# A hybrid encoder layer: the S5 phasors made during the projections and loaded in the attention loop

## The chip, the core and the metric

The kernel runs on one core of one Trainium2 chip. A core has five engines that work side by side, each through its own instructions in their order: TensorE (PE, matrix products; its weight loads are PEld), VectorE (DVE), ScalarE (ACT), GpSimd (POOL) and SyncE (SP), which here only issues DMAs. Engines wait for each other and for DMAs through semaphores; an instruction that waits holds up everything behind it on its engine. The metric is the device time of one execution in microseconds.

## The reference

One layer over 2048 positions of width 1024 (batch 1, depth 1). The normed input is projected once, and the columns are shared out among an attention branch, an S5 branch and their gates:

```
h = RMSNorm(x);  z = h @ w_in            # q 256, kv 128, k_rope 64, gate 512, u 512, gate 512
A = MLA attention, 4 heads, softmax over all 2048 positions
B = S5: 32 groups of 16 channels, 64 complex states each, forward and backward scan
    lam_bar = exp(lam * dt);  h_t = lam_bar * h_(t-1) + b_bar u_t;  y = Re(C h) + D u
B = gelu(B);  B = B * sigmoid(B @ w_glu + b_glu)
out = x + RMSNorm(concat(RMSNorm(A)*SiLU(gA), RMSNorm(B)*SiLU(gB)) @ w_out)
```

All is float32; products are made of three matmuls on split operands (`mm3`).

## The kernel before, in words

Every engine's order is written out by hand (`manual_schedule` for all five): what stands in the code is the order on each engine, and nothing is moved later.

**Projections** (about 0 to 380 us). The 16 position tiles go in pairs. For the pair starting at tile `s`, `blocks(s)` runs eight blocks of some 5.7 us on PE: z of the first tile, u (two), the attention gate `ga` (two), the S5 gate `gs` (two), z of the second tile; in the first and the last pair the two z blocks come first, side by side. After the seventh and eighth block `turn` transposes the next pair's two tiles into PSUM (`pt`, two buffers), and ACT and DVE copy each out as a rounded part `hh` and a rest `hl` (L195, L196). A gate block ends with a DVE operation `gst` (L330) and two stores. Each tile is normed with DVE `rv`, POOL `rr`, DVE `xt` (L188, L189, L268).

After each block from the second pair on, `step()` lets a generator go on with table work on DVE until a budget is used: each table operation charges 60 + its elements to a meter, each step takes `BUDGET` = 1800 off. The generator makes the rope tables first and then the S5 tables (`s5_params`), which it stores to `tab_d` in DRAM. There are 52 steps: eight in each of six pairs, four in the last.

**Attention loop** (about 395 to 1125 us). Steps `t` of some 2.7 us, eight to a unit (one head of 256 queries). In a step PE makes scores `sc` into one of two PSUM buffers (L1102 to L1106), transposes earlier probabilities (`pt`, L1150), and multiplies with the values (`av`); DVE takes the maximum (`nm`, L1107) and a rest `plo` (L1572); ACT takes the exponential `e` (L1113), which releases the scores' buffer, and the rounded copy `phi` (L1158). Into these steps the 32 S5 groups are woven, seven steps each (two take six), by `s5_pre` and `s5_post`. Every four groups form a set q with one table tile `tab` (two buffers), loaded from `tab_d` in the first step of the set before (`s5_load`, L858). In that set's third step `k_build(q)` issues 8 stores to `k_d` (L936, L937) and 8 loads `m` from it (L941).

In a group's third step POOL makes its phasors, cosine and sine over the 256 chunks, from four 16-element tables: two products (L971, L972) and, a step later, their sum (L975), into a tile `t` (`t3`, two buffers). In the fifth step ACT adds the negated copy (L984). DVE uses them two steps later (L997), POOL once more (L1018).

Then come the tail of the attention, the GLU and the output projection, which the change doesn't touch.

Of the kernel before, what the change touches and what calls it, by code (L numbers as in the profile page):

```python
# [11 lines left out]
F32 = mybir.dt.float32  # L12
# [4 lines left out]
ALU = mybir.AluOpType  # L17
# [28 lines left out]
LN2_2 = float(np.float32(math.log(2.0) - LN2_1))  # L46
GELU_C = math.sqrt(2.0 / math.pi)
GELU_A = 0.044715
BUDGET = 1800
MANUAL = {mybir.EngineType.PE, mybir.EngineType.Activation, mybir.EngineType.DVE, mybir.EngineType.Pool, mybir.EngineType.SP}  # L50


# [90 lines left out]
def bc(ap, dims):  # L143
    return ap.to_broadcast(dims)
# [3 lines left out]
def tile_hymba(ctx, tc, x, pos, inv_freq, pre_g, w_in, q_g, w_uqT, w_uqr, kv_g, w_ukT, w_uv, attn_g,  # L148
# [62 lines left out]
    for nm, m in ([("qr", T), ("qi", T)] + [(f"bt{i}", GH) for i in range(3)] + [("br", GH), ("bi", GH)]  # L211
# [2 lines left out]
        F[nm] = 4 * n_tab, m  # L214
        n_tab += m
    tab_d = dram.tile([P, NG // 4, 4 * n_tab], F32, tag="tab_d", name="tab_d")


    ph1, ph1a, ph1b, ph1g = (ExitStack() for _ in range(4))

    def pool(st, name, bufs, **kw):
        return st.enter_context(tc.tile_pool(name=name, bufs=bufs, reuse_waits="tile", **kw))
# [9 lines left out]
    s5t = pool(ph1g, "s5t", 7, side="right")  # L232
    xp = pool(ph1b, "xp", 2, side="right")
    s5p = pool(ph1b, "s5p", 1, side="right")
    psT = pool(ph1, "psT", 2, space=PSUM)
    psZ = pool(ph1, "psZ", 5, space=PSUM)
    psK = pool(ph1, "psK", 1, space=PSUM)
# [113 lines left out]
    def s5_params():  # L351
# [6 lines left out]
        def store(nm, ap):  # L358
            o, m = F[nm]
            G.dma_start(tab_d[:, :, o:o + 4 * m], ap.rearrange("p (q g) m -> p q (g m)", g=4))  # L360

        def neg(src, m):
            t_ = Scratch(s5t, [P, NG, m], "sc")()
            e.tensor_scalar(t_, src, -1.0, None, ALU.mult)
            return t_
# [85 lines left out]
        for nm, src in (("b", ph2), ("a", ph32)):  # L451
            hi, lo = new("hi" + nm), new("lo" + nm)
            e.tensor_scalar(hi, src, 1.5 * 2.0 ** 13, None, ALU.add)
            e.tensor_scalar(hi, hi, 1.5 * 2.0 ** 13, None, ALU.subtract)
            e.tensor_tensor(lo, src, hi, ALU.subtract)
            ang, rr = sp(), sp()
            ix = bc(idx[nm].unsqueeze(1), d3)
            e.tensor_tensor(ang, bc(hi.unsqueeze(2), d3), ix, ALU.mult)
            yield from reduce_angle(e, sp, rr, ang)
            e.tensor_tensor(ang, bc(lo.unsqueeze(2), d3), ix, ALU.mult)  # L460
            yield
            e.tensor_tensor(rr, rr, ang, ALU.add)
            yield
            if nm == "a":
                e.tensor_tensor(rr[:, :, 8:16], rr[:, :, 8:16], bc(phi.unsqueeze(2), [P, NG, 8]), ALU.add)
                r0, rr = rr, sp()
                yield from reduce_angle(e, sp, rr, r0)
            so, co = sp(), sp()
            yield from sincos(e, sp, so, co, rr)
            if nm == "a":  # L470
                e.tensor_copy(ep_r, co[:, :, 8])
                e.tensor_scalar(ep_i, so[:, :, 8], -1.0, None, ALU.mult)

            e.tensor_scalar(so[64:P], so[64:P], -1.0, None, ALU.mult)
            yield
            if nm == "b":
                store("bs", so)
                store("bc", co)
            else:
                store("aa3", so)  # L480
                store("aa2", co)
                store("aa1", neg(so, 16))
                store("aa0", neg(co, 16))
            yield

        br, bi = new("br", GH), new("bi", GH)
# [35 lines left out]
        yield from wait_steps(2)  # L522


        pc = psK.tile([P, 4, P], F32, tag="k", name="pc")
        rawn = neg(rawi, GH)
        yield from wait_steps(1)
# [8 lines left out]
        cst = Scratch(s5t, [P, 4, P], "sc")()  # L536
        for n in range(4):
            e.scalar_tensor_tensor(cst[:, n, :], ident, dsk[:, n:n + 1], pc[:, n, :], ALU.mult, ALU.add)
        for j in range(8):
            w = slice(GH * j, GH * j + GH)  # L540
            SP.dma_start(k_d[j::8, :, T, :].rearrange("n i h -> i n h"), cst[w, :, w])
# [6 lines left out]
        yield  # L548

    def tables():  # L550
        yield from rope_tables()
        yield from s5_params()

    gen = tables()

    def wait_steps(n):
        for _ in range(n):
# [3 lines left out]
    def step():  # L561

        VM.n -= BUDGET
        while VM.n < 0 and next(gen, "end") != "end":
            pass

    def blocks(s):

# [58 lines left out]
    for s in range(0, NT, 2):  # L627
        last = s + 2 == NT
        blk = blocks(s)
        for n in range(4 if last else 8):  # L630
# [13 lines left out]
                turn(xs[n - 6], n - 6)  # L644
            if s > 0:
                step()
    assert next(gen, "end") == "end"
    ph1b.close()
    ph1a.close()

# [299 lines left out]
    def group(g):  # L950

        q, i = divmod(g, 4)
        f = S5[q]

        uh, ul = (t_[:, :, i] for t_ in U)
        wt = s2.tile([P, 2, P], F32, tag="w", name="w")
        tmp = s2.tile([P, 2, P], F32, tag="tmp", name="tmp", bufs=2)
        two(G, wt, tmp, f["qr"][:, i, ::-1], f["qi"][:, i, ::-1], f["bt"][:, i, 1:3, :], f["bt"][:, i, 0:2, :])
        yield "pre"
        yield "post"  # L960
        G.tensor_tensor(wt, wt, tmp, ALU.add)
        yield "pre"
        yield "post"

        t3 = s2.tile([P, 3, 16, 16], F32, tag="t3", name="t3", bufs=2)
        t3b = s2.tile([P, 2, 16, 16], F32, tag="t3b", name="t3b")
        d = [P, 2, 16, 16]

        def b4(t):
            return bc(t[:, i, :].unsqueeze(1).unsqueeze(1), d)  # L970
        G.tensor_tensor(t3[:, 0:2], bc(f["aa"][:, i, 1:3, :].unsqueeze(3), d), b4(f["bc"]), ALU.mult)  # L971
        G.tensor_tensor(t3b, bc(f["aa"][:, i, 0:2, :].unsqueeze(3), d), b4(f["bs"]), ALU.mult)  # L972
        yield "pre"
        yield "post"
        G.tensor_tensor(t3[:, 0:2], t3[:, 0:2], t3b, ALU.add)  # L975
        t3 = t3.rearrange("p a b c -> p a (b c)")
        yield "pre"
        pw = psM.tile([P, 512], F32, tag="m", name="pw2")
        for ri in range(2):
            PE.transpose(pw[:, ri * P:(ri + 1) * P], wt[:, ri, :], ident)  # L980
        wh_, wl_ = (s2.tile([P, 256], F32R, tag=x_, name=x_) for x_ in ("wTh", "wTl"))
        split(wh_, wl_, pw[:, 0:256])
        yield "post"
        A.activation(t3[:, 2, :], t3[:, 0, :], AF.Copy, scale=-1.0)  # L984
        yield "pre"
        yield "post"
        yield "pre"
        px = psM.tile([P, 2, NC], F32, tag="m", name="px")
        for ri in range(2):
            w = slice(ri * P, (ri + 1) * P)  # L990
            mm3(px[:, ri, :], wh_[:, w], wl_[:, w], uh, ul, True, True)
        yield "post"
        d = [P, 2, NC]
        co, si = bc(t3[:, 1:2, :], d), t3[:, ::-2, :]
        ta = s2.tile(d, F32, tag="ta", name="ta")
        tb = s2.tile(d, F32, tag="tb", name="tb")
        V.tensor_tensor(ta, px, co, ALU.mult)  # L997
        V.tensor_tensor(tb, px[:, ::-1, :], si, ALU.mult)
        yield "pre"
        yield "post"  # L1000
        xm, gt = Xm[g % 2], Gt[g % 2]
        V.tensor_tensor(in_time(xm), of_tiles(ta), of_tiles(tb), ALU.add)
        yield "pre"
        yield "post"

        df = bc(f["rt"][:, i, :], [P, NC - 1])
        for r in range(2):
            o = r * NC
            V.tensor_tensor_scan(gt[0:64, o + 2:o + NC + 1], df[0:64], xm[0:64, r, 0:NC - 1], 0.0, ALU.mult, ALU.add)
            V.tensor_tensor_scan(gt[64:P, o + 1:o + NC][:, ::-1], df[64:P], xm[64:P, r, 1:][:, ::-1], 0.0,  # L1010
                                 ALU.mult, ALU.add)
            yield "pre"
            yield "post"
        g3 = gt[:, 1:2 * NC + 1].rearrange("p (a c) -> p a c", a=2)
        hc = s2.tile(d, F32, tag="hc", name="hc")
        tb2 = s2.tile(d, F32, tag="tb2", name="tb2")
        g4, co, si = in_time(g3), of_tiles(co), of_tiles(si)
        G.tensor_tensor(of_tiles(hc), g4, co, ALU.mult)  # L1018
        G.tensor_tensor(of_tiles(tb2), g4[:, ::-1], si, ALU.mult)
        yield "pre"  # L1020
        yield "post"
        G.tensor_tensor(hc, hc, tb2, ALU.subtract)
        yield "pre"
        yield "post"
        yield "pre"
        py = psY.tile([P, 2, P], F32, tag="y", name="py")
        mm3(py, M[0][:, i, :], M[1][:, i, :], uh, ul, True, False)
        yield "post"
        yield "pre"
        yield "post"  # L1030
        yield "pre"
        for ri in range(2):
            PE.matmul(py, f["v"][i][:, ri, :], hc[:, ri, :], start=False, stop=ri == 1)
        if i == 0:
            f["y"] = s1.tile([P, 2, 4, P], F32, tag="y4", name=f"y4_{q}")
        A.activation(f["y"][:, :, i, :], py, AF.Copy)
        if i == 3:
            for s8 in range(8):
                SP.dma_start(y_d[s8, q].rearrange("a (g h) c -> h (a g) c", g=4),
                             f["y"][s8 * GH:(s8 + 1) * GH].rearrange("h a g c -> h (a g) c"))  # L1040
        yield "end"
# [634 lines left out]
```

## Time and profile before

| | |
|---|---|
| median of 3 runs | 1387.77 us (1386.6 to 1389.01) |
| the profiled execution's own time | 1389.19 us |
| its span, first to last instruction | 1387.4 us |
| PE, DVE, ACT, POOL busy | 97%, 70%, 57%, 47% |
| chain that ended last, by engine | PE 78%, DVE 10%, ACT 4%, POOL 3%, DMA 1% |

A time is compared with the median. The profile is one execution, and durations and waits come from it. A busy share is a mean over stages with different limits, so a change is judged in the stage where it acts. A row of a timeline gives start, duration, engine, line, operation, the tiles as output<-input, and in square brackets the idle time before it and what ended it.

### The profile page before, as it was taken

The page shows a single profiled execution, that of the slowest core. Times are in us where ns is not written, and L with a number is a line of the kernel's source. Part 1 is how long each engine was busy: PE and PEld are TensorE (multiplying, and loading weights), DVE is VectorE, ACT ScalarE, POOL GpSimd, SP SyncE. Part 2 cuts the span into 40 slices and gives each one's busy share as a digit, 9 for nine tenths or more (in the row PEclk, how much of TensorE's full clock was granted, in tenths as well). Part 3 has the DMA queues.
Part 4 walks back from the last instruction along what each step waited for, and adds up shares of the span by engine and source line. Part 5 has one row for each costly group of instructions (what it writes and reads, how often), then busy time and mean ns, then how long its engine had stood idle before and what let it go on. Part 6 is the DMA issues. An engine that isn't in the chain of part 4 may idle for free.

```text
span 1387.4 us, 24305 instructions
## 1 busy us (share of the span) xinstructions
PE 1349.4 (97%) x9016; PEld 1219.0 (88%) x9016; DVE 974.4 (70%) x1812; ACT 797.4 (57%) x1828; POOL 647.7 (47%) x680
## 2 busy tenths in 40 slices
PE   7999999999989999999999999999999999999998
PEld 7999999999968888898888888888888887888886
DVE  6456554442388888887888788787887886767774
ACT  7312222222248778777778777777787785445442
POOL 2102320332357576565667655756641984333340
PEclk9999999999999999999999999999999999999999
DMA  8322323442630020201202021110101344455432
GB/s 299 88 54 76 83 68 83 87 123 62 157 83 21 27 45 9 51 24 29 46 5 63 12 45 31 28 39 10 29 9 43 105 116 110 141 171 167 130 106 92
DMA packets 122135, 102.93 MB, mean 74 GB/s; under 512 B 14672, under 2 KB 107104, under 8 KB 122016
## 3 DMA queue, kind: packets, MB, share of 16 engines
q1 hardware_dynamic: 110384, 89.43, 23.1%
q0 software_dynamic: 2272, 7.62, 2.2%
q10 hardware_dynamic: 9360, 4.33, 1.5%
q8 instruction: 70, 1.15, 0.4%
q14 instruction: 49, 0.40, 0.1%
HBM read 63.80 MB, written 37.54 MB: 73 GB/s over the span
## 4 chain that ended last, share of the span: by engine, by line
PE 78%; DVE 10%; ACT 4%; issue 3%; POOL 3%; DMA 1%; SPq 0%; POOLq 0%; ACTq 0%; DVEq 0%
PE pt L1150 6%; PE po L202 4%; PE po L203 4%; PE po L204 4%; PE sc L1102 3%; PE av L1170 3%; PE av L1171 3%; PE av L1172 3%; PE sc L1105 3%; PE sc L1103 3%; PE sc L1106 3%; PE sc L1104 3%; PE z_ga L203 2%; PE z_ga L204 2%; PE z_ga L202 2%
## 5 line engine op out<-in xcount | busy, mean ns | idle before, releaser
L1572 DVE TENSOR_TENSOR plo<-pt,phi 128x512 fp32r<-128x512 f32 x255 | 175.8, 689 | 80.9 <-ACT phi L1158 78.7
L1113 ACT ACTIVATE e<-sc,nm 128x512 f32<-128x512 f32 x256 | 176.8, 690 | 74.3 <-DVE nm L1107 73.2
L1158 ACT ACTIVATE phi<-pt 128x512 fp32r<-128x512 f32 x256 | 153.5, 600 | 80.7 <-PE pt L1150 79.2
L1107 DVE TENSOR_REDUCE nm<-sc 128x1 f32<-128x512 f32 x256 | 175.6, 686 | 25.8 <-PE sc L1106 22.3
L1170 PE MATMUL av<-phi,kn_h 128*128 128x256 f32 x512 | 165.2, 323 | 5.9 <-ACT avs L1175 5.9
L1142 ACT ACTIVATE e<-e,f 128x512 f32<-128x512 f32 x226 | 164.8, 729 | 1.5 <-DVE f L1131 1.5
L1150 PEld LDWEIGHTS pt<-ident,e 128*128 128x128 f32 x1024 | 127.4, 141 | 36.6 <-DVE e L1138 2.4
L1150 PE MATMUL pt<-ident,e 128*128 128x128 f32 x1024 | 154.5, 273 | 2.3 <-DVE e L1138 1.5
L1172 PE MATMUL av<-plo,kn_h 128*128 128x256 f32 x512 | 144.9, 283 | 0.4 <-DVE plo L1572 0.4
L1171 PE MATMUL av<-phi,kn_l 128*128 128x256 f32 x512 | 144.6, 283 | 0.0
L1102 PE MATMUL sc<-kT_h,qo 128*128 128x512 f32 x256 | 114.4, 447 | 6.6 <-ACT e L1113 4.9
L1018 POOL TENSOR_TENSOR hc<-G,t 128x512 f32<-128x512 f32 x32 | 41.7, 1304 | 153.5 <-DVE G L1010 140.0
L1170 PEld LDWEIGHTS av<-phi,kn_h 128*128 128x128 f32 x512 | 97.7, 191 | 8.5 <-ACT avs L1175 8.5
L202 PE MATMUL po<-woh,ah 128*128 128x512 f32 (+1 forms) x264 | 103.2, 391 | 1.9 <-ACT u L1409 1.9
L204 PE MATMUL po<-woh,al 128*128 128x512 f32 (+1 forms) x264 | 103.1, 390 | 0.0
L203 PE MATMUL po<-wol,ah 128*128 128x512 f32 (+1 forms) x264 | 103.0, 390 | 0.0
L1103 PE MATMUL sc<-kT_l,qo 128*128 128x512 f32 x256 | 101.2, 395 | 0.0
L1105 PE MATMUL sc<-krS,qo 128*128 128x512 f32 x256 | 101.0, 395 | 0.0
L1106 PE MATMUL sc<-krS,qo 128*128 128x512 f32 x256 | 100.9, 394 | 0.0
L1104 PE MATMUL sc<-kT_h,qo 128*128 128x512 f32 x256 | 100.2, 392 | 0.0
L1171 PEld LDWEIGHTS av<-phi,kn_l 128*128 128x128 f32 x512 | 97.5, 190 | 0.0
L1172 PEld LDWEIGHTS av<-plo,kn_h 128*128 128x128 f32 x512 | 96.6, 189 | 0.6 <-DVE plo L1572 0.6
(338 smaller groups left out, 4105.3 us busy)
## 6 DMA issues: line engine op xcount, KB each, us to landing
g_d<-gst SPq DMA_DIRECT2D x64, 128.0 KB, 2.0
g<-g_d SPq DMA_DIRECT2D x16, 512.0 KB, 5.9
xr<-in_x_dram SPq DMA_DIRECT2D x16, 512.0 KB, 6.5
xt<-in_x_dram SPq DMA_DIRECT2D x15, 512.0 KB, 3.8
out_dram<-res SPq DMA_DIRECT2D x15, 512.0 KB, 3.0
u_d<-ust ACTq DMA_DIRECT2D x64, 64.0 KB, 2.1
u<-u_d SPq DMA_DIRECT2D x64, 64.0 KB, 2.5
o_d<-o SPq DMA_DIRECT2D x32, 128.0 KB, 1.8
```

Source lines behind the costliest of these rows:

```text
L202: PE.matmul(ps, ahi, bhi, start=first, stop=False)
L203: PE.matmul(ps, ahi, blo, start=False, stop=False)
L204: PE.matmul(ps, alo, bhi, start=False, stop=last)
L1102: PE.matmul(ps, qo[:, 0, w], kT_h[:, c], start=True, stop=False)
L1107: V.tensor_reduce(st["nm"][:, qt, kb:kb + 1], ps, AX.X, ALU.max, negate=True)
L1113: A.activation(e, st.pop("s"), AF.Exp, bias=st["nm"][:, qt, kb:kb + 1], accum_out=st["L"][:, qt, kb:kb + 1])
L1142: A.activation(e, e, AF.Copy, scale=f)
L1150: PE.transpose(pt[:, kk, qt, :], st["e"][qt, kt // 4][:, o:o + P], ident)
L1170: PE.matmul(o, kn_h[:, kt, :], hi[:, w], start=kt == 0, stop=False)
L1171: PE.matmul(o, kn_l[:, kt, :], hi[:, w], start=False, stop=False)
L1172: PE.matmul(o, kn_h[:, kt, :], lo[:, w], start=False, stop=kt == NT - 1)
L1572: V.tensor_tensor(lo[0], lo[1], f32(lo[2]), ALU.subtract)
```

## The change

In the projections a second generator, `phasors`, makes the phasors of all 32 groups and stores them to a new DRAM tensor `ph_d`. For every set of four it loads the tables into a tile `pht`. For each group POOL makes one product into `ph`, DVE the other into PSUM (`phb`, in the single buffer of `psK`) and their sum into `ph`, and SP stores it, 256 KB. `ph` and `pht` have one buffer each. `step()` calls this generator once after the tables that it needs are stored, twice when the other generator has run dry, and not while `psK` is held by another product. The budget goes from 1800 to 2300, and the S5 tables come ahead of the rope tables.

In the attention loop the two products and the sum of a group go, and in their place SP loads the tile `t` from `ph_d`.

```diff
-BUDGET = 1800
+BUDGET = 2300
...
+    ph_d = dram.tile([NG, P, 2, 256], F32, tag="ph_d", name="ph_d")
...
+    php = pool(ph1b, "php", 1, side="right")
...
                 store("aa0", neg(co, 16))
+                made.append(True)
...
+        held.append(True)
         pc = psK.tile([P, 4, P], F32, tag="k", name="pc")
...
             e.scalar_tensor_tensor(cst[:, n, :], ident, dsk[:, n:n + 1], pc[:, n, :], ALU.mult, ALU.add)
+        held.clear()
...
     def tables():
+        yield from s5_params()
         yield from rope_tables()
-        yield from s5_params()
-
-    gen = tables()
+
+    made, held = [], []
+
+    def phasors():
+
+        d = [P, 2, 16, 16]
+        for q in range(NG // 4):
+            tb = php.tile([P, 5, 4, 16], F32, tag="pht", name="pht")
+            o = F["aa0"][0]
+            SP.dma_start(tb[:, 0:3].rearrange("p r g m -> p (r g m)"), tab_d[:, q, o:o + 192])
+            o = F["bc"][0]
+            SP.dma_start(tb[:, 3:5].rearrange("p r g m -> p (r g m)"), tab_d[:, q, o:o + 128])
+            yield
+            for i in range(4):
+                t2 = php.tile(d, F32, tag="ph", name="ph")
+                t2b = psK.tile(d, F32, tag="k", name="phb")
+
+                def b4(r):
+                    return bc(tb[:, r, i, :].unsqueeze(1).unsqueeze(1), d)
+                G.tensor_tensor(t2, bc(tb[:, 1:3, i, :].unsqueeze(3), d), b4(3), ALU.mult)
+                V.tensor_tensor(t2b, bc(tb[:, 0:2, i, :].unsqueeze(3), d), b4(4), ALU.mult)
+                V.tensor_tensor(t2, t2, t2b, ALU.add)
+                SP.dma_start(ph_d[4 * q + i], t2.rearrange("p r a c -> p r (a c)"))
+                if i < 3:
+                    yield
+
+    gen, phs = tables(), phasors()
...
     def step():
         VM.n -= BUDGET
         while VM.n < 0 and next(gen, "end") != "end":
             pass
+        for _ in range((bool(made) + (VM.n < 0)) * (not held)):
+            next(phs, None)
...
-        t3 = s2.tile([P, 3, 16, 16], F32, tag="t3", name="t3", bufs=2)
-        t3b = s2.tile([P, 2, 16, 16], F32, tag="t3b", name="t3b")
-        d = [P, 2, 16, 16]
-
-        def b4(t):
-            return bc(t[:, i, :].unsqueeze(1).unsqueeze(1), d)
-        G.tensor_tensor(t3[:, 0:2], bc(f["aa"][:, i, 1:3, :].unsqueeze(3), d), b4(f["bc"]), ALU.mult)
-        G.tensor_tensor(t3b, bc(f["aa"][:, i, 0:2, :].unsqueeze(3), d), b4(f["bs"]), ALU.mult)
+        t3 = s2.tile([P, 3, 256], F32, tag="t3", name="t3", bufs=2)
+        SP.dma_start(t3[:, 0:2, :], ph_d[g])
         yield "pre"
         yield "post"
-        G.tensor_tensor(t3[:, 0:2], t3[:, 0:2], t3b, ALU.add)
-        t3 = t3.rearrange("p a b c -> p a (b c)")
         yield "pre"
```

Two places show how instructions move. The first is DVE in the projections' seventh pair (tiles 12 and 13), from the norm of the second tile loaded (`rv`, `xt`) on; `gst` are the gates. Before:

```order
L188 TENSOR_SCALAR rv<-ss 128x1
L268 TENSOR_SCALAR xt_3451<-xt_3451,rr 128x1024
L68 TENSOR_SCALAR sc<-sc 128x512
L330 SCALAR_TENSOR_TENSOR gst<-tt,z_ga 128x512 x2
L68 TENSOR_SCALAR sc<-sc 128x512
L330 SCALAR_TENSOR_TENSOR gst<-tt,z_gs 128x512 x2
L196 TENSOR_TENSOR hl<-pt,hh 128x4x128 x2
```

DVE at the same place now:

```order
L188 TENSOR_SCALAR rv<-ss 128x1
L270 TENSOR_SCALAR xt_3615<-xt_3615,rr 128x1024
L579 TENSOR_TENSOR phb<-pht 128x512
L580 TENSOR_TENSOR ph<-ph,phb 128x512
L579 TENSOR_TENSOR phb<-pht 128x512
L580 TENSOR_TENSOR ph<-ph,phb 128x512
L332 SCALAR_TENSOR_TENSOR gst<-tt,z_ga 128x512
L579 TENSOR_TENSOR phb<-pht 128x512
L580 TENSOR_TENSOR ph<-ph,phb 128x512
L579 TENSOR_TENSOR phb<-pht 128x512
L580 TENSOR_TENSOR ph<-ph,phb 128x512
L332 SCALAR_TENSOR_TENSOR gst<-tt,z_ga 128x512
```

Two phasors now stand behind the second norm and behind each gate; from the first norm of this pair up to the transposed copies `hl` there are ten, in five steps, and six more follow in three steps. The sixteen phasors before them come one to a step.

The second place is SP at the first group of a set in the attention loop (set 6 here): `tab` the next set's tables, `k_d` and `m` the stores and loads of `k_build`, `o_d` the attention's output. Before:

```order
L858 DMA tab_10165<-tab_d 128x964
L936 DMA k_d<-ks 16x128
L937 DMA k_d<-ks 16x128
...
L941 DMA m_10269<-k_d 16x4x128 x8
L1182 DMA o_d<-o 128x2x128
```

SP at the same place now, `t` being the phasors:

```order
L891 DMA tab_10326<-tab_d 128x964
L969 DMA k_d<-ks 16x128
L970 DMA k_d<-ks 16x128
...
L974 DMA m_10430<-k_d 16x4x128 x8
L999 DMA t_10441<-ph_d 128x512
L1207 DMA o_d<-o 128x2x128
```

The load of the group's phasors stands behind the tables' load and the sixteen DMAs of `k_build`. It is so in the first group of sets 1 to 6; in set 7 there is no tables' load ahead.

## Rows read from the trace of the kernel before

**Rows 1.** Two stages: us; busy us of PE, PEld, DVE, ACT, POOL; PEclk; DMA share; GB/s.

```profile
100.00:330.00 230.00, 230.00 (x1775) 225.80 (x1773) 113.38 (x309) 51.96 (x120) 53.66 (x72) 1.00 0.35 87
396.00:1082.00 686.00, 671.72 (x4457) 593.36 (x4456) 561.90 (x1031) 521.83 (x1238) 416.05 (x433) 1.00 0.13 31
```

**Rows 2.** Waits of SP's queue: who waited for whom, us, times, longest.

```profile
SPq L858 <- DVE G L1010: 92.4, 6, 22.0
...
SPq L936 <- ACT ks L932: 12.2, 2, 11.5
```

**Rows 3.** Timeline of SP, first group of set 1.

```profile
481.90 0.34 SPq L858 DMA_DIRECT2D tab<-tab_d  x1
...
482.81 0.41 SPq L936 DMA_DIRECT2D k_d<-ks  x1
...
487.56 3.61 SPq L941 DMA_DIRECT2D m<-k_d  x8
```

**Rows 4.** Timeline of SP, first group of set 6.

```profile
897.35 3.62 SPq L941 DMA_DIRECT2D m<-k_d  x8
```

**Rows 5.** Timeline of ACT, first groups of sets 1 and 6.

```profile
486.33 0.42 ACT L984 ACTIVATE t<-t 128x256 f32<-128x256 f32 x1
...
487.32 0.68 ACT L1113 ACTIVATE e<-sc,nm 128x512 f32<-128x512 f32 x1
...
897.52 0.43 ACT L984 ACTIVATE t<-t 128x256 f32<-128x256 f32 x1
...
898.30 0.71 ACT L1113 ACTIVATE e<-sc,nm 128x512 f32<-128x512 f32 x1
```

**Rows 6.** Timeline of PE: scores two steps after those copies; a pause at 838.06.

```profile
491.36 0.40 PE L1102 MATMUL sc<-kT_h,qo 128*128 128x512 f32 x1
...
838.06 0.50 PE L1102 MATMUL sc<-kT_h,qo 128*128 128x512 f32 x1 [2.45 <-ACT e L1113]
...
902.72 0.39 PE L1102 MATMUL sc<-kT_h,qo 128*128 128x512 f32 x1
```

**Rows 7.** Stretches behind that pause, columns as in rows 1.

```profile
838.88:842.28 3.40, 3.40 (x16) 3.11 (x15) 2.44 (x4) 3.40 (x10) 3.40 (x6) 0.50 0.14 40
842.30:845.70 3.40, 3.40 (x25) 3.09 (x25) 2.36 (x4) 1.53 (x4) 3.32 (x5) 1.00 0.02 5
```

**Rows 8.** DMA issues: count, KB each, median us from issue to landing.

```profile
wuv<-in_w_uv_dram SPq DMA_DIRECT2D x1, 256.0 KB, 2.6
...
out_dram<-res SPq DMA_DIRECT2D x1, 256.0 KB, 2.0
...
zr<-z_d SPq DMA_DIRECT2D x4, 128.0 KB, 3.6
...
sc<-in_c_re_dram SPq DMA_DIRECT2D x1, 256.0 KB, 3.9
```

**Rows 9.** Groups of instructions, 396 to 1082 us: count | busy, mean ns | idle before.

```profile
L975 POOL TENSOR_TENSOR t<-t,t3b 128x512 f32<-128x512 f32 x32 | 42.0, 1312 | 0.2
...
L971 POOL TENSOR_TENSOR t<-tab 128x512 f32<-128x512 f32 x32 | 38.6, 1205 | 0.0
...
L972 POOL TENSOR_TENSOR t3b<-tab 128x512 f32<-128x512 f32 x32 | 37.1, 1159 | 0.0
...
L1002 DVE TENSOR_TENSOR X<-ta,tb 128x512 f32<-128x512 f32 x32 | 25.4, 795 | 0.0
...
L997 DVE TENSOR_TENSOR ta<-px,t 128x512 f32<-128x512 f32 x32 | 21.9, 685 | 6.5 <-PE px L204 6.1 <-POOL tmp L906 0.5
...
L984 ACT ACTIVATE t<-t 128x256 f32<-128x256 f32 x32 | 13.7, 427 | 6.3 <-POOL t L975 6.3
```

**Rows 10.** Timeline of the seventh pair: first norm on DVE, last transposes on PE.

```profile
305.02 0.76 DVE L268 TENSOR_SCALAR xt<-xt,rr 128x1024 f32<-128x1024 f32 x1 [0.70 <-POOL rr L189]
...
334.94 1.03 PE L276 MATMUL pt<-ident,xt 128*128 128x128 f32 x8
```

**Rows 11.** Chain of waits, 321.5 to 323.6 us: start, us, what.

```profile
321.78 1.78 PE pc L531 x16
```

More of the change, by code (lines that the diff above doesn't have):

```diff
@@ L646, in tile_hymba @@
                 step()
-    assert next(gen, "end") == "end"
+    assert next(gen, "end") == "end" and next(phs, "end") == "end"
     ph1b.close()
```

## The prediction

> **What bounds the kernel now.** The stretches by stage come first: in the projections PE is busy in 230.00 of 230.00 us, in the attention loop in 671.72 of 686.00, at the full clock in both, while POOL has 416.05 of 686.00 in the loop [rows 1]. So POOL work taken out of the loop can give back no more than the 686.00 − 671.72 = 14.3 us in which PE has nothing to do there. The rest of the reading is for what the change can make PE wait for. The waits of SP's queue show that SP stands still for a set's tables 6 times, 92.4 us in all, until DVE's scan L1010 has let go of the old ones, but only twice for the `ks` copy behind them [rows 2]. The timelines of SP, ACT and PE around those places, and of the seventh pair of the projections, give the distances from which stalls are worked out. The list of DMA issues and the groups of instructions give the durations.
>
> **What leaves the loop.** Per group two products and a sum on POOL, 1205 + 1159 + 1312 ns [rows 9], or 3.68 us, 32 times: 117.7 us of POOL. PE gains by it only where it waits for POOL, or for a DVE or ACT that POOL delays. ACT's copy L984 has waited 6.3 us in all for the sum [rows 9]. DVE is slower beside POOL: `X` (L1002), with both inputs in SBUF, takes 795 ns, and `ta` (L997), of the same shape with one input from PSUM, 685 [rows 9]; 32 × 110 ns is 3.5 us, and the scans are stretched likewise. The Trainium skill says the same, in "GPSIMD Engine Reference", Specifications: the SBUF interfaces are shared with VectorE, and DVE instructions with two SBUF inputs contend there. By that rule alone the change would be a gain, and the rows agree with the rule; but they limit it to the 14.3 us. Bounds: 0, and 14.3 if all of PE's idle time went. I take 5, a third, since three of some thirteen POOL instructions of a group go.
>
> **What comes into the loop.** A load of 256 KB per group on SP, issued in the group's third step and needed by ACT's copy in its fifth. In the first group of sets 1 to 6 it stands behind the tables' load and the sixteen DMAs of `k_build`. In set 1 the tables were issued at 481.90, when the scan had released them; the first store `k_d` went at 482.81, and the eight loads `m` took SP from 487.56 for 3.61 us, to 491.17 [rows 3]. The load can go at 491.2. A 256 KB load took 2.6 us (`wuv`) to 3.9 us (`c_re`) to land [rows 8]; I take 2.8, near the one with no load issued beside it. It lands at 494.0; the copy started at 486.33 [rows 5]: ACT waits 7.7 us. In set 6: 897.35 + 3.62 = 900.97 [rows 4], landing 903.8, copy at 897.52 [rows 5]: 6.3 us. These are the first and the last of six; the mean is 7.0. In set 7 nothing waits for tables, so I count none; the other 25 groups have two steps of 2.7 us for 2.8 us.
>
> Behind the copy on ACT stand `phi` and the exponential `e`, and `e` must release the scores' buffer before PE can write the scores two steps on. In set 1 `e` ended at 487.32 + 0.68 = 488.0 and those scores started at 491.36: 3.4 us of slack; in set 6 at 899.0 and 902.72: 3.7 us [rows 5, 6]. PE so loses 7.0 − 3.5 = 3.5 us. DVE waits too, since its `plo` waits for `phi`, and the next maximum stands behind it; I add 0.5, less than one DVE operation. 6 × 4.0 = 24 us. Bounds: with a landing of 2.6 and no DVE term 6 × 3.3 = 20; with 3.9 and a DVE operation or two more 6 × 6 = 36.
>
> A pause has a second price. PE stood 2.45 us for `e` before 838.06 [rows 6], and in the stretch from 838.88 to 842.28 the granted clock was 0.50: 16 matmuls instead of the 25 of the next stretch of the same length at 1.00 [rows 7]. Nine matmuls at 3.40/25 us are 1.2 us. Six pauses of about 4 us, longer than that one, cost 6 × 1.2 = 7 us more (0 to 10). The Trainium skill, "TensorE: Matmul & The Clock Gate", Part 1, has the throttled state as the default, which activity releases; that speaks against this change wherever PE stands still, and the row agrees. Loop: 24 + 7 − 5 = +26.
>
> **What comes into the projections.** 32 products on POOL, 64 operations on DVE, 32 stores and 16 small loads. With one phasor to a step, DVE has some 2.4 us of tables, 1.4 of phasor and a gate of 0.7 in a step of 5.7 us; it was busy in 113.38 of 230.00 us [rows 1], so these sixteen lie under PE and cost nothing. If that cover fails it is at the first one, which waits for the tables' stores: up to 3 us.
>
> The sixteen of the last eight steps come by twos, and the tile `ph` has one buffer: POOL's product waits until the store before has landed, DVE's sum waits for the product, the store for the sum. One round is a store of 256 KB, 2.0 us (`out_dram`, same size [rows 8]), a product of 1.2 (L971) and a sum of 0.69 (as L997) [rows 9], with 0.2 for three hand-overs: 4.1 us. Each fourth round waits for a set's `pht` tables instead, two more issues and a read of at most 3.6 us (`zr` [rows 8]): 1.5 us more. Two rounds make 8.2 us in a step of 5.7, so DVE falls behind, and what stands behind the sums in its queue are the gates and then `hl`, without which PE's next z block can't run.
>
> Counted in the times of before: the first norm on DVE ended at 305.78 [rows 10]. Behind it come the last rope operation (0.4), `phb` and the sum (0.69 each): 307.6 for the first of ten. Nine more rounds, two with new tables: 307.6 + 9 × 4.1 + 2 × 1.5 = 347.5. Gate and first half of `hl` (0.69 each): 348.9. PE's second transposes need a buffer that `hl` releases; they came at 334.94 [rows 10], less the 1.78 us of `pc` [rows 11], which is now made earlier: 333.2. PE stands 15.7 us. Two more phasors (8.2 us) stand before the second tile's `hl`, against some 6.4 us of transposes, z block and `hl` work: 2 us more. Four more follow before the last z block's norm; DVE has caught up when the gates of the last pair come, four blocks later. With 1.2 us for the clock: 15.7 + 2 + 1.2 = +19. Bounds: rounds of 3.8 and 1.0 for tables give 13; rounds of 4.5 and 2.2 give 24, and 3 for the first wait.
>
> **The sum.** +19 + 26 = +45, on the profiled 1389.19 (span 1387.4): 1434. That execution was 1.4 us over the median of 1387.77, so 1433 beside the median.
>
> **Rivals.**
> 1. Only the projections lose. ACT's wait would have to stay within its slack. For it: ACT is busy in 521.83 of 686.00 us [rows 1] and can catch up. Against: 7.0 exceeds 3.5 at both places read. Then 1387.8 + 19 − 5 = 1402.
> 2. Only the loop loses. It needs a round of at most 2.9 us, two to a step; the store and product alone are 3.2. 1387.8 + 26 = 1414.
> 3. More than forecast: after each wait DVE (561.90 of 686.00 us) has `phi`'s rests, maxima and group products to make up and PE stops again, and the first phasor's wait for the table stores reaches PE: 6 × 7 + 10 − 3 + 27 = +76, or 1464.
> 4. Not slower: POOL's relief decides. The mechanism is PE's idle time in the loop, worth up to 14.3 us, at the places where POOL's product holds up a scan of DVE or the copy of ACT. It decides only if the loads land before the fifth step, which SP's order forbids in six places, and if sixteen rounds fit into eight steps. 1387.8 − 8 = 1380.
> 5. The phasors are not made ahead but late: the loads of groups 0 and 1 waiting for stores of the last pair. The stores of set 0 are some 100 us earlier; without price, and given no chance.
>
> **How the numbers follow.** The forecast (both losses) has 0.68, rival 1 0.11, rival 2 0.08, rival 3 0.09, rival 4 0.04. The forecast's own range is 1412 to 1456. For 8 in 10 I go from 1403, which takes in rival 2 and nearly rival 1, to 1460; left out are most of rival 3, rival 1's lower half and rival 4. About 0.2% is what a measurement of this kernel can tell from no change; faster by more 0.03, within it 0.02, slower 0.95.
>
> **What the next profile would show.** In the waits of ACT a new row, copy `t` (now L1009) for the DMA `t<-ph_d`, about 42 us in 6 pieces, in place of the 6.3 us for POOL; pauses of PE before `sc` right after, with a granted clock of 0.50 behind them. In the seventh pair DVE waiting for POOL's `ph`, POOL for the DMA `ph_d<-ph`, and PE idle for some 16 us before its second transposes; the loop starting some 19 us later. POOL in the loop about 118 us less busy. If ACT's copies wait under 3 us, or PE stays busy through the last two pairs, the forecast is wrong at that step; if the loop is shorter than before, in its main point.

## The result, and the profile after

The changed kernel takes 1455.11 us (median of 4 runs, 1449.79 to 1457.44) against 1387.58 before: ratio 1.0481, 95% interval 1.0466 to 1.0495. It is 67.5 us slower where 45 were forecast; the range, 1403 to 1460, holds it. The profiled execution took 1457.44 us, its span 1455.6, which is 68.2 more than the span before; it is the slowest of the four, so stages read from it add up to a little more than the medians differ by.

PE runs the same 9016 matmuls in both kernels, and all but the sixteen of `pc` in the same order. So the others can be put side by side one by one, and the distance between the two starts tells where the loss arises:

| matmul (before, after) | after is later by | what came on since the row above |
|---|---|---|
| `z` 201.68, 204.34 | 2.7 us | a pause at 106 us, 1.8 |
| `z` 236.59, 245.42 | 8.8 | 1.8 of it `pc`, which now stands here and no longer at 321.8; the rest a pause before it and half clock |
| `z` 289.26, 302.75 | 13.5 | a pause at 299 us, and half clock |
| `z_gs` 323.32, 335.43 | 12.1 | `pc` is gone from its old place |
| `z` 336.63, 368.35 | 31.7 | the pause before the second transposes of the seventh pair |
| `py` 430.55, 464.66 | 34.1 | the start of the loop |
| `sc` 903.65, 972.62 | 69.0 | six pauses in the first groups of sets 1 to 6 |

So the projections and the start of the loop lose 34 us (forecast 19), the loop 35 (forecast 26). The first figure differs between executions: the five kernels here that share these projections (`after`, `load_first`, `load_mid`, `tab_late`, `proj_only`) have lost 30 to 35 us when the loop starts.

The stretches by stage, with the columns of [rows 1]: the projections up to the pause, the pause, the loop.

```profile
100.00:347.00 247.00, 239.92 (x1800) 233.25 (x1798) 143.96 (x263) 52.04 (x119) 80.40 (x89) 0.99 0.40 109
347.00:365.10 18.10, 0.14 (x1) 0.00 (x0) 7.54 (x13) 2.81 (x8) 4.72 (x4) 0.62 0.32 104
429.10:1150.90 721.80, 684.35 (x4460) 602.99 (x4459) 551.83 (x1034) 521.66 (x1238) 302.46 (x338) 0.97 0.17 41
```

In the loop POOL has 302.46 us instead of 416.05, 113.6 less (117.7 forecast), and PE stands for 721.80 − 684.35 = 37.5 us instead of 14.3. The waits, in us, times and longest:

```profile
DVE ph L580 <- POOL ph L578: 56.2, 25, 4.8
...
POOL ph L578 <- DMA ph_d<-ph: 50.8, 16, 5.6
ACT t L1009 <- DMA t<-ph_d: 45.7, 7, 8.0
...
PE pt L278 <- DVE hl L196: 22.6, 3, 18.0
...
DVE phb L579 <- DMA pht<-tab_d: 17.0, 7, 6.2
```

All the rows named beforehand are there. The third is the copy's wait: 45.7 us, in place of the 6.3 for POOL [rows 9].

**The loop.** SP in the first group of set 1, which answers to [rows 3]:

```profile
516.31 0.32 SPq L891 DMA_DIRECT2D tab<-tab_d  x1
...
517.20 0.41 SPq L969 DMA_DIRECT2D k_d<-ks  x1
...
521.89 3.62 SPq L974 DMA_DIRECT2D m<-k_d  x8
525.62 0.36 SPq L999 DMA_DIRECT2D t<-ph_d  x1
```

ACT and PE there, to [rows 5, 6]; in brackets the idle time ahead and what ended it:

```profile
528.39 0.42 ACT L1009 ACTIVATE t<-t 128x256 f32<-128x256 f32 x1 [7.54 <-DMA t<-ph_d]
528.71 0.58 ACT L1183 ACTIVATE phi<-pt 128x512 fp32r<-128x512 f32 x1
529.19 0.68 ACT L1138 ACTIVATE e<-sc,nm 128x512 f32<-128x512 f32 x1
```

```profile
530.01 0.80 PE L1127 MATMUL sc<-kT_h,qo 128*128 128x512 f32 x1 [4.09 <-ACT e L1138]
```

The load is issued 9.3 us after the tables' (481.90 to 491.2 in the forecast, as much), and 2.8 us later the copy starts; ACT stands 7.54 us (7.7 forecast) and PE 4.09. The granted clock behind the pause, columns of [rows 1]:

```profile
530.00:535.50 5.50, 5.49 (x18) 4.72 (x19) 5.02 (x10) 3.98 (x9) 2.98 (x4) 0.50 0.01 3
535.60:539.00 3.40, 3.40 (x23) 3.04 (x23) 1.80 (x4) 2.92 (x7) 2.37 (x3) 1.00 0.14 39
618.40:624.30 5.90, 5.89 (x19) 5.01 (x20) 5.47 (x13) 5.42 (x12) 0.00 (x0) 0.50 0.00 1
969.60:972.40 2.80, 2.80 (x10) 2.51 (x11) 2.05 (x4) 2.74 (x6) 0.00 (x0) 0.50 0.19 53
```

PE runs at the lower of its two levels, 1.2 GHz, for 5.5 us after this pause of 4.09, for 5.9 after the second (4.22) and for 2.8 after the last (3.62); in [rows 7] it was 3.4.

**The projections.** The tile `ph` from 322 to 366 us: its instructions with shortest, median and longest ns, then what their engines waited for:

```profile
L578 POOL TENSOR_TENSOR ph<-pht x10: 1053/1060/1569, 321.7 to 362.1; 128x512 f32<-128x512 f32 x10
L580 DVE TENSOR_TENSOR ph<-ph,phb x10: 687/689/689, 323.4 to 363.2; 128x512 f32<-128x512 f32 x10
...
  DMA ph_d<-ph: 20.8, 7
  POOL ph L578: 19.1, 9
  DMA pht<-tab_d: 10.9, 3
```

Ten sums from 323.4 to 363.2 are nine rounds of 4.42 us. Two of them hold a wait for new tables; the third such wait came before the first sum. Behind the last sum stand a gate and `hl`, and behind `hl` PE:

```profile
321.72 1.60 DVE L579 TENSOR_TENSOR phb<-pht 128x512 f32<-128x512 f32 x1 [2.21 <-DMA pht<-tab_d]
```

```profile
365.11 1.97 PE L278 MATMUL pt<-ident,xt 128*128 128x128 f32 x8 [17.97 <-DVE hl L196]
```

Before this the phasors come one to a step, and there too a store came late. On SP it follows the loads of C:

```profile
231.80 0.44 SPq L521 DMA_DIRECT2D sc<-in_c_re_dram  x1
232.29 1.19 SPq L522 DMA_DIRECT2D sc<-in_c_im_dram  x1
234.78 0.33 SPq L581 DMA_DIRECT2D ph_d<-ph  x1
```

POOL waits 5.62 us for it to land, DVE 4.78 for POOL, and gates and `hl` stand behind:

```profile
239.65 1.05 POOL L578 TENSOR_TENSOR ph<-pht 128x512 f32<-128x512 f32 x1 [5.62 <-DMA ph_d<-ph]
```

```profile
240.74 0.69 DVE L580 TENSOR_TENSOR ph<-ph,phb 128x512 f32<-128x512 f32 x1 [4.78 <-POOL ph L578]
241.34 0.68 DVE L332 SCALAR_TENSOR_TENSOR gst<-tt,z_gs 128x512 f32<-128x512 f32 x1
...
242.28 0.68 DVE L332 SCALAR_TENSOR_TENSOR gst<-tt,z_gs 128x512 f32<-128x512 f32 x1
242.87 1.28 DVE L196 TENSOR_TENSOR hl<-pt,hh 128x512 fp32r<-128x512 f32 x2
```

```profile
241.48 0.49 PE L535 MATMUL pc<-sc,br 128*128 128x128 f32 x2 [1.88 <-DVE ph L580]
...
299.39 1.69 PE L278 MATMUL pt<-ident,xt 128*128 128x128 f32 x8 [3.02 <-DVE hl L196]
```

At 241.48 the matmul `pc` waits for the buffer of `psK`, which the phasor held until that sum; at 299.39 the transposes wait for `hl`, which stands behind a phasor that had waited on DVE for its tables (1.35 us) and for POOL (0.94).

**What POOL's absence gives.** The groups of DVE in the loop, to [rows 9] (count | busy, mean ns):

```profile
L1027 DVE TENSOR_TENSOR X<-ta,tb 128x512 f32<-128x512 f32 x32 | 22.9, 715 | 0.0
...
L1022 DVE TENSOR_TENSOR ta<-px,t 128x512 f32<-128x512 f32 x32 | 21.9, 683 | 4.6 <-PE px L204 4.5
```

`X`, with both inputs in SBUF, falls from 795 to 715 ns; `ta`, with one input in PSUM, stays at 685 and 683. By the Trainium skill ("GPSIMD Engine Reference", Specifications) it is the first kind that contends with POOL; the trace agrees.

### The profile page after: what moved, and what is told of

It reads as the page before. It is cut to its first block, busy times and chain, and to the rows that moved or that the text cites. A ratio compares the mean times of both kernels' runs of the same rounds, so it can differ in the third digit from the quotient of the medians.

```text
span 1455.6 us, 24546 instructions
## 1 busy us (share of the span) xinstructions
PE 1367.1 (94%) x9016; PEld 1231.0 (85%) x9016; DVE 1011.3 (69%) x1876; ACT 797.1 (55%) x1828; POOL 571.3 (39%) x616
## 3 DMA queue, kind: packets, MB, share of 16 engines
q8 instruction: 70, 1.15, 0.3%
## 4 chain that ended last, share of the span: by engine, by line
PE 48%; DVE 11%; DMA 6%; ACT 5%; POOL 4%; issue 4%; SPq 3%; POOLq 0%; ACTq 0%; DVEq 0%
PE pt L1175 5%; PE po L202 4%; PE po L203 4%; PE po L204 4%; PE sc L1127 3%; PE av L1195 3%; PE sc L1128 3%; PE sc L1130 3%; PE sc L1129 3%; PE sc L1131 3%; PE av L1196 3%; PE av L1197 3%; DMA ph_d<-ph 2%; DVE nm L1132 2%; PE py L1058 2%
## 5 line engine op out<-in xcount | busy, mean ns | idle before, releaser
L1127 PE MATMUL sc<-kT_h,qo 128*128 128x512 f32 x256 | 116.9, 457 | 27.7 <-ACT e L1138 25.0
L1129 PE MATMUL sc<-kT_h,qo 128*128 128x512 f32 x256 | 102.1, 399 | 0.0
```

Of the source, the lines that this page charges most:

```text
L1127: PE.matmul(ps, qo[:, 0, w], kT_h[:, c], start=True, stop=False)
```

## The experiments

All medians are compared with runs of the kernel before on the same chip (1387.25 to 1387.94 us). By the intervals, the difference between two variants is uncertain by some 2 to 3 us.

**1. The load first (`load_first`).** The tile and its load go from the group's third step to its first, and the set's table load behind them.

```diff
+        t3 = s2.tile([P, 3, 256], F32, tag="t3", name="t3", bufs=2)
+        SP.dma_start(t3[:, 0:2, :], ph_d[g])
         tmp = s2.tile([P, 2, P], F32, tag="tmp", name="tmp", bufs=2)
         two(G, wt, tmp, f["qr"][:, i, ::-1], ...
...
-                if i == 0 and q < 7:
-                    s5_load(q + 1)
...
         for x_ in live:
             next(x_)
+        if g >= 0 and o == 0 and i == 0 and q < 7:
+            s5_load(q + 1)
```

> The changed kernel with one thing moved: the load of a group's phasors is issued in the group's first step, ahead of the next set's table load, so that no SP wait for DVE's scan and none of the sixteen DMAs of k_build stand before it. My theory (SP's order in the first group of six sets costs the loop): ACT's copy waits for this DMA under 3 us in all instead of 45.7, the six pauses of PE before the scores (4.4 to 5.4 us each, and about 2 us each at half clock) go, and the kernel comes to 1455 - 36 = 1419 us (1414 to 1424). Rival (the 256 KB loads are late by their landing or by what they share with other DMAs, wherever they stand): the copy still waits over 20 us, and the time stays above 1438.

1414.03 us, ratio to before 1.0187 (1.0173 to 1.0201): 41.1 us less than the changed kernel. In set 1:

```profile
505.51 0.34 SPq L991 DMA_DIRECT2D t<-ph_d  x1
516.04 0.32 SPq L891 DMA_DIRECT2D tab<-tab_d  x1
```

```profile
520.51 0.42 ACT L1009 ACTIVATE t<-t 128x256 f32<-128x256 f32 x1
```

The load goes 10.5 us ahead of the tables', and the copy waits for nothing. SP's order was the cause, and the six pauses with their half clock cost 41 us, 5 more than expected.

**2. A ring for the phasors (`two_buffers`).** Order unchanged on every engine.

```diff
-            tb = php.tile([P, 5, 4, 16], F32, tag="pht", name="pht")
+            tb = php.tile([P, 5, 4, 16], F32, tag="pht", name="pht", bufs=2)
...
-                t2 = php.tile(d, F32, tag="ph", name="ph")
+                t2 = stg.tile(d, F32, tag="st", name="ph")
```

> The changed kernel with other buffers for making the phasors: the phasor goes through the ring of eight staging tiles that outputs use, and the small table tile has two buffers. The order on every engine is the same. My theory (single buffers make product, sum and store take turns): POOL's wait for the store (50.8 us) falls under 10, the 18 us pause of PE before the second transposes of the seventh pair and the 6.2 us one at 239 us go, and with the 3 to 5 us at 299 the time comes to 1455 - 27 = 1428 us (1423 to 1435). Rival (DVE has too much to do in the last two pairs, sixteen phasors of 1.4 us on top of gates and splits, or waits for the small table loads): PE still pauses over 10 us there and the time stays above 1440.

1435.23 us, 1.0343 (1.0329 to 1.0357): 19.9 less, at the upper edge of what was expected. POOL's wait for the stores is gone. The pause is not:

```profile
POOL ph L578 <- DMA pht<-tab_d: 43.3, 8, 12.7
...
DVE ph L580 <- POOL ph L578: 22.7, 12, 4.3
```

```profile
344.84 1.97 PE L278 MATMUL pt<-ident,xt 128*128 128x128 f32 x8 [5.12 <-DVE hl L196]
```

17.97 became 5.12 us. The single buffer made most of it; the rest is waits for `pht`, whose loads stand behind the store of the set before.

**3. Both (`both`).** Edits 1 and 2.

> Both edits together: the early load and the ring of staging tiles. My theory: the two losses lie in different stages and add up, so the gains of the single edits (36 and 27) add too: 1455 - 63 = 1392 us (1385 to 1398), with some 3 us of the projections left and POOL's relief in the loop worth little. Rival 1 (POOL's relief is worth much, up to the 14.3 us in which PE had nothing to do): under 1384. Rival 2 (the stalls overlap, one taking over when the other goes): above 1402.

1394.49 us, 1.0047 (1.0033 to 1.0061). Alone the edits give 41.1 and 19.9, together 60.6: the two losses are in different stages and add up. 6.5 us are left.

**4. Behind the tables, ahead of `k_build` (`load_mid`).** The two lines go to the end of the group's second step.

```diff
         G.tensor_tensor(wt, wt, tmp, ALU.add)
         yield "pre"
         yield "post"
-
-        t3 = s2.tile([P, 3, 256], F32, tag="t3", name="t3", bufs=2)
-        SP.dma_start(t3[:, 0:2, :], ph_d[g])
...
+        t3 = s2.tile([P, 3, 256], F32, tag="t3", name="t3", bufs=2)
+        SP.dma_start(t3[:, 0:2, :], ph_d[g])
+        G.tensor_tensor(wt, wt, tmp, ALU.add)
```

> The changed kernel with the load of the phasors one step earlier: behind the next set's table load, which waits for DVE's scan, but ahead of the sixteen DMAs of k_build. My theory (the 9.7 us that the sixteen DMAs take on SP are what makes it late; released by the scan at about 0.5 us after the table load, the load lands some 3.3 us later, before the copy): the copy waits under 6 us in all and the time is within 4 us of the kernel with the load in the first step, 1419 to 1423. Rival (the wait for the scan alone is enough): ACT still waits over 20 us and the time stays above 1435.

1414.98 us, 1.0194 (1.0180 to 1.0207): within 4 us of `load_first`, as expected, though 4 us under the figures named, since `load_first` itself came out faster. The copy hardly waits:

```profile
ACT t L1009 <- DMA t<-ph_d: 0.6, 1, 0.6
```

SP's wait for the scan alone does no harm: the sixteen DMAs must be added to it.

**5. The tables late (`tab_late`).** The other half of that pair: now the scan's wait goes and the sixteen DMAs stay.

```diff
-                if i == 0 and q < 7:
-                    s5_load(q + 1)
...
+        if g >= 0 and o == 2 and i == 0 and q < 7:
+            s5_load(q + 1)
```

> The changed kernel with the next set's table load moved behind the load of the phasors (third step instead of first). The phasors' load still stands behind the sixteen DMAs of k_build, but no longer behind SP's wait for the scan; the copy ks, which these need, was ready 3.9 to 5.1 us before the table load was released (512.06 against 516.31 in set 1). My theory (wait and DMAs add up, and PE feels only what exceeds ACT's slack of 3.4 us): the copy waits 7.3 - 4.3 = 3.0 us in each of six sets, some 18 us in all instead of 45.7, PE's pauses go but for some tenths, and the time comes to 1415 us (1412 to 1421), near the kernel with the early load, though ACT still waits. Rival (the sixteen DMAs alone are enough to stop PE): 1430 or more.

1423.14 us, 1.0265 (1.0243 to 1.0288), 2 us over the range expected. In sum the copy waits about as forecast, 19.4 us where 18 were expected, but unevenly (7 times, 1.9 to 5.01):

```profile
522.01 0.42 ACT L1009 ACTIVATE t<-t 128x256 f32<-128x256 f32 x1 [5.01 <-DMA t<-ph_d]
```

```profile
523.64 0.49 PE L1127 MATMUL sc<-kT_h,qo 128*128 128x512 f32 x1 [1.56 <-ACT e L1138]
...
691.19 0.51 PE L1127 MATMUL sc<-kT_h,qo 128*128 128x512 f32 x1 [1.65 <-ACT e L1138]
```

Where ACT waits 5.0 and 4.1 us (sets 1 and 3) PE pauses 1.6; at the five waits of 1.9 to 2.3 it doesn't; at 7.54 it paused 4.09. That is a slack of 2.5 to 3.5 us; the prediction had 3.5. The late tables made a new wait, for POOL's next `v`:

```profile
POOL v L938 <- DMA tab<-tab_d: 30.2, 6, 6.9
```

Whether it costs PE anything isn't shown. Of PE's other pauses those at 620 us (1.69) and 873 us (1.41) aren't new: `load_first` has them too, 1.57 and 1.35. New are 0.79 at 785 us and most of 1.15 at 788 (0.36 in `load_first`). The two pauses at copies and these make some 5 of the 9 us by which this kernel is slower than `load_first`; the rest comes in pieces under 1 us that were not traced.

**6. Only the projections' half (`proj_only`).** The loop is that of before: POOL makes the phasors again, and what the projections store is not read.

```diff
-        t3 = s2.tile([P, 3, 256], F32, tag="t3", name="t3", bufs=2)
-        SP.dma_start(t3[:, 0:2, :], ph_d[g])
+        t3 = s2.tile([P, 3, 16, 16], F32, tag="t3", name="t3", bufs=2)
+        t3b = s2.tile([P, 2, 16, 16], F32, tag="t3b", name="t3b")
...
```

> The changed kernel with the attention loop of before: the phasors are made and stored in the projections as in the change, but nobody loads them, and POOL makes them again in the loop. My theory: the projections' part costs what the start of the loop shows, 32 to 34 us, so 1388 + 33 = 1421 us (1416 to 1425); against the kernel with the early load (1414), the difference is what POOL's relief is worth in the loop, 7 us (4 to 10). Rival (the relief is worth nothing, or the loads cost as much): within 2 us of 1414. Rival (part of the projections' loss comes from the loop's loads): under 1410.

1418.17 us, 1.0230 (1.0213 to 1.0247). The loop starts 35.0 us later than before, about as in the changed kernel (34), so its loads have no part in that loss. Against `load_first` (1414.03) it is 4.1 us slower by the medians and 6, give or take 3, by the ratios; in the traces the loop of `load_first` gains 7.1 us against before, this one 2.7, which is 4.4 less. POOL's relief is worth some 4 us, where the prediction took 5 of 14.3.

**7. Only the tables' order and budget (`tables_only`).** The kernel before with two edits.

```diff
-BUDGET = 1800
+BUDGET = 2300
...
     def tables():
+        yield from s5_params()
         yield from rope_tables()
-        yield from s5_params()
```

> The kernel before, with the budget of 2300 and the rope tables last, and no phasors at all. My theory (of the 32 us lost in the projections, the 1.8 us pause at 104 us, and about 2 of those at 239 us, where DVE stands for the load of C, come from the new order of the table work and not from phasors; the matmul pc, now under cover, gives 1.5 back): 1388 + 2.5 = 1390.5 us (1388 to 1393). Rival (all comes from the phasors): within 1 us of 1388, or below for the freed 1.8 us of pc.

1389.27 us, 1.0016 (1.0008 to 1.0025): 2.0 us. It is the pause at 106 us, where PE waits for `hl`:

```profile
105.79 1.25 PE L276 MATMUL pt<-ident,xt 128*128 128x128 f32 x8 [1.72 <-DVE hl L196]
```

The two edits weren't tried apart, so whether the larger budget or the new order makes it is open. No pause is seen at 240 us. What I had read as one, 2 us by which the later matmuls are late, is `pc`, which has been moved there.

**8. The next tables ahead (`tables_ahead`).** `both`, with each set's `pht` loads issued before the third phasor of the set before.

```diff
+        nxt = load(0)
+        yield
         for q in range(NG // 4):
+            tb = nxt
             for i in range(4):
+                if i == 2 and q < 7:
+                    nxt = load(q + 1)
```

> The kernel with both edits (1394.5 us), and the small tables of the next set of phasors loaded one phasor earlier, ahead of the third of a set instead of behind the fourth. Left in it is a 5.4 us pause of PE before the second transposes of the seventh pair. My theory (DVE's waits of 3.7 and 2.6 us for these loads, which stand behind the stores on SP, put it late there): the waits of DVE for pht fall from 17.8 us to under 3, the pause and its 1.4 us at half clock go, and the time is 1394.5 - 7 = 1387.5 us (1385 to 1391). Rival (DVE simply has too much work in these eight steps, two phasors, a gate and rope work in 5.7 us): the pause stays above 4 us and the time above 1392.

1386.77 us, 0.9998 (0.9989 to 1.0006), 7.7 under `both`. PE doesn't pause in the seventh pair any more, though DVE's waits for `pht` fell only to 6.4 us (under 3 expected), 6.1 of them at the first phasor. DVE had time enough for two phasors, a gate and `hl` in a step; it lacked data. The change, so mended, is worth nothing measurable: the loop gains 6.9 us from 399 to 995 us of the kernel before, and that pays for what the projections still lose. Some 4 of it are POOL's relief (experiment 6). `proj_only`, without that relief, gains 2.7 as well, 2.5 of it at the pause at 838 us [rows 6]. Part of that comes from no edit at all: in the profiled execution of the kernel before, half clock followed that pause [rows 7]; in `tables_only` nearly the same pause has none behind it.

```profile
839.11 0.50 PE L1102 MATMUL sc<-kT_h,qo 128*128 128x512 f32 x1 [2.31 <-ACT e L1113]
```

```profile
839.20:842.60 3.40, 3.40 (x23) 3.08 (x24) 2.38 (x5) 3.40 (x9) 3.40 (x5) 1.00 0.25 72
```

**9. to 11. Three tries at the rest (`pool_half`, `c_earlier`, `all_three`)**, on `tables_ahead`. The first gives every second phasor to POOL alone:

```diff
-                t2b = psK.tile(d, F32, tag="k", name="phb")
+                sole = i % 2 == 0
+                t2b = (stg if sole else psK).tile(d, F32, tag="st" if sole else "k", name="phb")
...
-                V.tensor_tensor(t2b, ...
-                V.tensor_tensor(t2, t2, t2b, ALU.add)
+                (G if sole else V).tensor_tensor(t2b, ...
+                (G if sole else V).tensor_tensor(t2, t2, t2b, ALU.add)
```

> The kernel tables_ahead (1386.8 us), with every second phasor made by POOL alone (two products and the sum, 3.7 us, its scratch tile from the staging ring), so that DVE has 0.7 us of phasor work a step on the mean and 1.4 where two are made. My theory (what is left at 204 and 293 us, 0.6 and 1.6 us, is DVE being late for hl behind table work and phasors): those two go, 1386.8 - 2 = 1384.8 us (1383 to 1387). Rival (POOL, slow and now asked for 4.8 us in a step with two phasors, is late itself for the stores and for rr of the norms): 1389 or more.

1391.12 us, 1.0029 (1.0020 to 1.0039), 4.3 us slower than `tables_ahead`: the rival's time. POOL is now the late one; these four sums of DVE wait for it, and PE pauses behind the last:

```profile
327.12 0.69 DVE L589 TENSOR_TENSOR ph<-ph,phb 128x512 f32<-128x512 f32 x1 [2.19 <-POOL ph L587]
...
331.88 0.69 DVE L589 TENSOR_TENSOR ph<-ph,phb 128x512 f32<-128x512 f32 x1 [2.19 <-POOL ph L587]
...
336.63 0.69 DVE L589 TENSOR_TENSOR ph<-ph,phb 128x512 f32<-128x512 f32 x1 [2.20 <-POOL ph L587]
...
342.41 0.69 DVE L589 TENSOR_TENSOR ph<-ph,phb 128x512 f32<-128x512 f32 x1 [3.33 <-POOL ph L587]
```

```profile
344.35 1.25 PE L278 MATMUL pt<-ident,xt 128*128 128x128 f32 x8 [2.31 <-DVE hl L196]
```

Side by side with `tables_ahead`, 2.5 us come on there. Another 2.8 come on at 241 us, where `pc` waits 2.05 us for the negated copy of C on DVE.

The second gives the load of C more time:

```diff
+        dsk = s5p.tile([P, 4], F32, tag="dsk", name="dsk")
+        SP.dma_start(dsk, s5_d)
         SP.dma_start(rawr, c_re)
...
+        yield from wait_steps(1)
         held.append(True)
...
-        dsk = s5p.tile([P, 4], F32, tag="dsk", name="dsk")
-        SP.dma_start(dsk, s5_d)
-        yield from wait_steps(2)
+        yield from wait_steps(1)
```

> The kernel tables_ahead, with the negated copy of C one step later behind its load, the small load of D ahead of it, and one step less behind the matmul pc, so that the table work ends in the same step. My theory (1.9 us of PE at 240 us are lost because DVE stands 3 us for the load of C, with gate and hl behind it): that pause goes, 1386.8 - 1.9 = 1384.9 us (1383.5 to 1386.5). Rival (DVE is late there in any case): within 0.7 us of 1386.8.

1387.45 us, 0.9999 (0.9990 to 1.0008): no gain, since there was no pause to remove. `pc` now stands at 246.0 us instead of 238.8, and the 1.8 us by which later matmuls are late have gone there with it.

> Both edits on tables_ahead. If they add up, 1386.8 - 2 - 1.9 = 1382.9 us (1381 to 1385), 0.3% under the kernel before: the loop's gain of 7 us, less the 1.4 us that the order of the table work costs at 105 us. If they don't, above 1385.

1390.76 us, 1.0025 (1.0015 to 1.0034): by its time the loss of the first alone, but its pauses stand elsewhere, 3.17 us at 294 and 3.20 at 407 us and none at 344, so why these phasors on POOL cost 4 us is only partly shown. No version was found that is faster than the kernel before.

## Why the prediction was right, and where its sizes were off

**Right: both mechanisms, their places and their order of size.** The copy behind the tables' load and `k_build`: six waits of 6.24 to 7.98 us, 7.3 on the mean (7.0 forecast), and one of 1.83 in set 7, which PE doesn't feel; 45.7 us in all (42 forecast). Taking the load out of that queue gives 41 us back. The rounds over a single buffer: 4.42 us with two table waits among nine, as forecast (4.43). The pause behind them: 17.97 us (15.7 forecast), 2.3 more because the first of the ten also waited for new tables, 2.21 us, which the prediction's count left out. POOL's relief: some 4 us (5 forecast).

**The total is less exact than the mechanisms.** It came out half as large again as forecast. The forecast's own range, 1412 to 1456, holds 1455 by a single microsecond, and that is luck: the projections lost 34 us, outside the 13 to 27 that their bounds allowed, and the loop lost 35 where its sum gave 26. Two terms were too small.

**Too small: the price of a pause.** At the six pauses in the loop the matmuls fall back 3.8 to 5.3 us, 27.5 together where 24 were forecast: ACT's slack, taken as 3.5 us, was 2.5 to 3.5. Behind them they fall back a further 1.4 to 2.7 us each, 12.3 together, where 7 were forecast from the one stretch of [rows 7]. There the lower clock held for 3.4 us; after these pauses it held for 2.8 to 5.9. And counting matmuls of unlike sizes, 16 against 25, had put that stretch at 1.2 us; put side by side with `tables_only`, where the clock stayed up, it cost 1.6. Together 40, near the 41 that `load_first` gave back; about 5 of it returned between the sets, which is how the loop comes to a net 35.

**Wrong: "these sixteen lie under PE and cost nothing".** That step set the busy share of DVE, 113.38 of 230.00 us [rows 1], against the work added. But a phasor in DVE's queue doesn't only work there; it waits for POOL, which waits for the store before it, or for its tables. The table of displacements puts this stretch at 12.1 us up to 323 us: 1.6 to 1.9 at 106 us from the tables' order and budget (experiment 7), 4.3 at 240 and 5.0 at 299 us from phasors with the half clock behind them, and some tenths elsewhere. In five executions of the same projections the stretch came to 8.6 to 12.1 us; with the ring of buffers (`two_buffers`), the order on DVE unchanged, it is 4.7. So the single buffers make most of it, not the work. A store of 256 KB, 2.1 us in the median, landed 4.7 us after its issue at 235 us, behind the loads of C; the prediction had taken 2.0 for every one. The bound "up to 3 us" for the first phasor's wait looked at one that cost PE 0.5.

**Wrong: "two more phasors before the second tile's `hl`: 2 us".** Nothing came there; a single pause held all.

**Rivals.** Of the forecast's terms both losses came, so rivals 1, 2 and 4 are out (`proj_only` and `load_first` show each loss alone). Rival 3, 1464, was nearest in size, but not by its mechanism: the surplus is 15 us in the projections, mostly at their first sixteen phasors (2.4 come on at the start of the loop, 1.5 of them at half clock, and were not followed up), and 9 in the loop, 5 of it clock and 3.5 the pauses themselves. No further pauses beside the six were added in the loop, as DVE catching up would have made.

## What to carry to other kernels

A load that takes over from computation is only as early as its place in the issuing queue: count what stands ahead of it there, the wait of the first and the issue time of the rest, and move the load ahead of both, which gave 41 of the 67 us back here at no cost that shows. A producer with one buffer ran here at product + sum + store landing, and an in-order engine that takes part in it hands that wait to everything behind it; its busy share doesn't show this. When two traces are put side by side, a matmul that is later by the length of work which has merely moved ahead of it is not a pause: look for the idle time itself.

## What the runs showed of the hardware that I had not expected

After a pause of 4.09 us PE stayed at the lower clock level for 5.5 us, so that the pause cost more than half as much again (2.7 us); by the Trainium skill ("TensorE: Matmul & The Clock Gate", Part 1) the throttled state is the default and activity releases it, which the row agrees with. This price isn't fixed by the length of the pause: behind 2.45 us the granted clock fell to 0.50 in the kernel before [rows 6, 7], behind 2.31 us at the same matmul in `tables_only` it stayed at 1.00, and behind only 1.88 us before 241.48 in the changed kernel it fell again (0.50 from 242.1 to 245.4). And the landing of one store of 256 KB, issued 32 times from the same line, ranged from 2.0 to 4.7 us. The 4.7 came 2.5 to 3 us behind the issue of two loads of C, 256 KB each, which took 6.5 us to land; behind two equally large loads of B at the same distance, which took 2.9 and 3.0, the store landed in 2.0. What makes the difference was not tried.
